# Group-mean subtraction: hand-set semaphores per slot, sums alternating between SBUF and PSUM, and slots moved to multiples of 1 KiB

## Chip, cores, metric

One core of one Trainium2 chip. The metric is device time in microseconds (us) of one execution; a second number, the span, is what the profiler saw inside one execution (about 1.8 us less here). Runs of the kernel before agree within 0.1%.

## The reference

```python
def setup_inputs():
    B, S, D = 8, 4096, 2112
    return {"x": np.random.randn(B, S, D).astype(np.float32)}

def reference(x):                      # stride = 4
    x_r = x.reshape(B, S // stride, stride, D)
    pooled = x_r.mean(axis=2)
    upsampled = np.repeat(pooled, stride, axis=1)
    return (x - upsampled).astype(np.float32)
```

Every group of four rows loses its mean. 276.8 MB have to be read and 276.8 MB written; the arithmetic is small.

## The kernel before

A partition holds one group of four rows: 4 x 2112 float32 values, 33,792 bytes, contiguous both in HBM and in SBUF. A tile is 128 groups; there are 64 tiles. A slot, below, is one of the six tile buffers in SBUF.

```python
STRIDE = 4
IO_BUFS = 6
...
    io_pool = ctx.enter_context(tc.tile_pool(name="io", bufs=IO_BUFS))
    sum_pool = ctx.enter_context(tc.tile_pool(name="sum", bufs=1))

    for g0 in range(0, G, P):
        gsz = min(P, G - g0)
        x_tile = io_pool.tile([P, W], mybir.dt.float32)
        nc.sync.dma_start(out=x_tile[:gsz], in_=xg[g0:g0 + gsz])
        rows = x_tile[:gsz].rearrange("p (f d) -> p f d", f=STRIDE)
        s = sum_pool.tile([P, D], mybir.dt.float32)
        nc.vector.tensor_add(out=s[:gsz], in0=rows[:, 0, :], in1=rows[:, 1, :])
        for f in range(2, STRIDE):
            nc.vector.tensor_add(out=s[:gsz], in0=s[:gsz], in1=rows[:, f, :])
        nc.vector.scalar_tensor_tensor(      # rows = -s/4 + rows, in place
            out=rows, in0=s[:gsz, None, :].to_broadcast([gsz, STRIDE, D]),
            scalar=-1.0 / STRIDE, in1=rows,
            op0=mybir.AluOpType.mult, op1=mybir.AluOpType.add,
        )
        nc.scalar.dma_start(out=og[g0:g0 + gsz], in_=x_tile[:gsz])
```

Loads are issued by SyncE (queue q1 in the profile), stores by ScalarE (queue q10). The tile framework sets all semaphores and chooses the order of VectorE's instructions.

Of the kernel before, what the change touches and what calls it, by code (L numbers as in the profile page):

```python
# [1 line left out]

# [4 lines left out]

STRIDE = 4
IO_BUFS = 6  # L10


@with_exitstack
def kernel(
    ctx: ExitStack,
    tc: tile.TileContext,
    x: bass.AP,
    out: bass.AP,
):



    nc = tc.nc
    B, S, D = x.shape
    P = nc.NUM_PARTITIONS
    assert S % STRIDE == 0
    G = (B * S) // STRIDE
    W = STRIDE * D

    xg = x.rearrange("b (g f) d -> (b g) (f d)", f=STRIDE)  # L30
    og = out.rearrange("b (g f) d -> (b g) (f d)", f=STRIDE)

    io_pool = ctx.enter_context(tc.tile_pool(name="io", bufs=IO_BUFS))
    sum_pool = ctx.enter_context(tc.tile_pool(name="sum", bufs=1))

    for g0 in range(0, G, P):
        gsz = min(P, G - g0)
        x_tile = io_pool.tile([P, W], mybir.dt.float32)
        nc.sync.dma_start(out=x_tile[:gsz], in_=xg[g0:g0 + gsz])

        rows = x_tile[:gsz].rearrange("p (f d) -> p f d", f=STRIDE)
        s = sum_pool.tile([P, D], mybir.dt.float32)
        nc.vector.tensor_add(out=s[:gsz], in0=rows[:, 0, :], in1=rows[:, 1, :])  # L43
        for f in range(2, STRIDE):
            nc.vector.tensor_add(out=s[:gsz], in0=s[:gsz], in1=rows[:, f, :])  # L45
        nc.vector.scalar_tensor_tensor(  # L46
            out=rows,
            in0=s[:gsz, None, :].to_broadcast([gsz, STRIDE, D]),
            scalar=-1.0 / STRIDE,
            in1=rows,  # L50
            op0=mybir.AluOpType.mult,
            op1=mybir.AluOpType.add,
        )
        nc.scalar.dma_start(out=og[g0:g0 + gsz], in_=x_tile[:gsz])


# [1 line left out]
_INS = ['x']  # L58
_OUTS = [((8, 4096, 2112), 'float32')]


# [23 lines left out]
```

## Time and profile before

| | before |
|---|---|
| time, median of 3 | 1286.44 us |
| span | 1284.7 us |
| DMA, mean over the span | 431 GB/s |
| VectorE (DVE) busy | 1026.1 us, 80% |
| VectorE waiting for loads | 237.3 us |

Parts 1 to 3 of the page of the kernel before. In the rows of 40 each digit is the busy share of one slice of the span in tenths.

```profile
span 1284.7 us, 674 instructions
DVE 1026.1 (80%) x256; POOL 0.2 (0%) x4
DVE  5998778787787877878778787787887878778784
DMA  9999999999999999999999999999999999999998
GB/s 404 421 438 438 433 425 437 438 427 432 437 437 426 435 437 431 429 437 437 431 428 438 437 431 429 437 436 432 428 438 436 430 430 437 437 426 433 438 431 380
DMA packets 18437, 553.70 MB, mean 431 GB/s; under 512 B 2048, under 2 KB 2048, under 8 KB 2048
q1 hardware_dynamic: 9216, 276.83, 50.0%
q10 hardware_dynamic: 9216, 276.83, 49.9%
q14 instruction: 5, 0.04, 0.0%
```

The DMA row is at 9 in 39 of 40 slices and the two queues' packets fill the 16 engines' time (50.0% + 49.9%): the DMA engines hardly ever rest. Next, the groups of VectorE instructions (count | busy us, mean ns | idle before and what ended it), then VectorE's waits (total us, times, longest).

```profile
L46 DVE SCALAR_TENSOR_TENSOR x_tile<-s,x_tile 128x8448 f32<-128x8448 f32 x64 | 573.3, 8958 | 2.2
L43 DVE TENSOR_TENSOR s<-x_tile 128x2112 f32<-128x2112 f32 x64 | 150.9, 2358 | 237.5 <-DMA x_tile<-in_x_dram 237.3
L45 DVE TENSOR_TENSOR s<-s,x_tile 128x2112 f32<-128x2112 f32 x128 | 301.8, 2358 | 4.4
```

```profile
DVE s L43 <- DMA x_tile<-in_x_dram: 237.3, 59, 13.1
```

A tile costs VectorE 2.358 + 2 x 2.358 + 8.958 = 16.03 us and the DMA engines 1284.7 / 64 = 20 us. So VectorE waits for loads 59 times, about 4 us per tile, and has that much to spare. One view misleads:

```profile
## 4 chain that ended last, share of the span: by engine, by line
DVE 80%; another core or an unknown queue 17%; DMA 1%; issue 1%; DVEq 0%
```

The chain that ended last runs through VectorE because each of its waits ends with a load. That the load was late because the engines were full is not in the chain; it is in the DMA row.

The packed trace also has every DMA packet's start and duration. From these records: 16,384 data packets of 33,792 bytes, which makes 1024 per engine, from 1.75 us to 1283.56 us. Nearly every one (98.6% within 1 ns) is recorded as 1251 ns long, loads and stores alike.

### The profile page before, as it was taken

How to read it: one execution, taken by the hardware profiler on the slowest of the kernel's cores; microseconds unless marked ns; L12 is line 12 of the kernel's file. 1: busy time of each engine (PE TensorE's matmuls, PEld its weight loads, DVE VectorE, ACT ScalarE, POOL GpSimd, SP SyncE). 2: the span in 40 equal slices, each digit the busy share in tenths (PEclk: the TensorE clock that was granted, in tenths of full speed). 3: DMA queues.
4: the chain of work that ended last, by engine and by line, in shares of the span. 5: the costliest groups of instructions: out<-in, count | busy, mean ns of one | idle time of the engine just before them, and what ended most of it. 6: DMA issues, size and time to landing. Idle time of an engine off the chain costs nothing.

```text
span 1284.7 us, 674 instructions
## 1 busy us (share of the span) xinstructions
DVE 1026.1 (80%) x256; POOL 0.2 (0%) x4
## 2 busy tenths in 40 slices
DVE  5998778787787877878778787787887878778784
POOL 0000000000000000000000000000000000000000
DMA  9999999999999999999999999999999999999998
GB/s 404 421 438 438 433 425 437 438 427 432 437 437 426 435 437 431 429 437 437 431 428 438 437 431 429 437 436 432 428 438 436 430 430 437 437 426 433 438 431 380
DMA packets 18437, 553.70 MB, mean 431 GB/s; under 512 B 2048, under 2 KB 2048, under 8 KB 2048
## 3 DMA queue, kind: packets, MB, share of 16 engines
q1 hardware_dynamic: 9216, 276.83, 50.0%
q10 hardware_dynamic: 9216, 276.83, 49.9%
q14 instruction: 5, 0.04, 0.0%
HBM read 276.82 MB, written 276.82 MB: 431 GB/s over the span
## 4 chain that ended last, share of the span: by engine, by line
DVE 80%; another core or an unknown queue 17%; DMA 1%; issue 1%; DVEq 0%
DVE x_tile L46 45%; DVE s L45 24%; DVE s L43 12%; DMA x_tile<-in_x_dram 1%; DVEq L43 0%
## 5 line engine op out<-in xcount | busy, mean ns | idle before, releaser
L46 DVE SCALAR_TENSOR_TENSOR x_tile<-s,x_tile 128x8448 f32<-128x8448 f32 x64 | 573.3, 8958 | 2.2
L43 DVE TENSOR_TENSOR s<-x_tile 128x2112 f32<-128x2112 f32 x64 | 150.9, 2358 | 237.5 <-DMA x_tile<-in_x_dram 237.3
L45 DVE TENSOR_TENSOR s<-s,x_tile 128x2112 f32<-128x2112 f32 x128 | 301.8, 2358 | 4.4
L69 POOL MEMSET const-bfloat16-1.0<- 128x1 bf16 x1 | 0.1, 103 | 0.0
L69 POOL MEMSET const-uint8-127<- 128x1 uint8 x1 | 0.1, 102 | 0.0
L69 POOL MEMSET const-float32-0.0<- 128x1 f32 x1 | 0.1, 100 | 0.2 <-issue 0.2
L69 POOL MEMSET const-float32-1.0<- 128x1 f32 x1 | 0.1, 99 | 0.0
## 6 DMA issues: line engine op xcount, KB each, us to landing
x_tile<-in_x_dram SPq DMA_DIRECT2D x64, 4224.0 KB, 59.6
out_dram<-x_tile ACTq DMA_DIRECT2D x64, 4224.0 KB, 43.8
```

What stands on the lines that cost most here:

```text
L43: nc.vector.tensor_add(out=s[:gsz], in0=rows[:, 0, :], in1=rows[:, 1, :])
L45: nc.vector.tensor_add(out=s[:gsz], in0=s[:gsz], in1=rows[:, f, :])
L46: nc.vector.scalar_tensor_tensor(out=rows, in0=s[:gsz, None, :].to_broadcast([gsz, STRIDE, D]), scalar=-1.0 / STRIDE, in1=rows, op0=mybir. ...
L69: nc = _bacc.Bacc("TRN2", target_bir_lowering=False, num_devices=1)
```

## The change

Its intent: one fixed program per queue, with one semaphore per slot and direction, so that a load waits for its own slot's store alone; two sum buffers, so that a tile's first add needs no wait for the previous tile's subtraction; and slots at multiples of 1 KiB instead of 128 bytes past a multiple of 256. The second sum buffer lies in PSUM because I took SBUF to have no room for it beside the six slots.

The diff, cut to its core:

```diff
-    for g0 in range(0, G, P):
-        x_tile = io_pool.tile([P, W], mybir.dt.float32)
-        nc.sync.dma_start(out=x_tile[:gsz], in_=xg[g0:g0 + gsz])
-        s = sum_pool.tile([P, D], mybir.dt.float32)
 ...
+    pad_pool.tile([P, PAD], f32, name="pad")                # PAD = 224: 896 bytes
+    slots = [io_pool.tile([P, W], f32, name=f"slot{b}") for b in range(SLOTS)]
+    s_sb = sum_pool.tile([P, D], f32, name="s_sb")
+    s_ps = psum_pool.tile([P, D], f32, name="s_ps")
+    load_sems = [tc.alloc_semaphore(f"load{b}") for b in range(SLOTS)]
+    store_sems = [tc.alloc_semaphore(f"store{b}") for b in range(SLOTS)]
+    done_sem = tc.alloc_semaphore("done")
+    with tc.tile_critical():
+        done = 0
+        for k in range(n):
+            b, lap = k % SLOTS, k // SLOTS
+            s = s_ps if k % 2 else s_sb
+            load = nc.sync.dma_start(out=slots[b][:], in_=xg[tile_rows])
+            if lap:
+                load._wait_ge(store_sems[b], 16 * lap)
+            load.then_inc(load_sems[b], 16)
+            add = nc.vector.tensor_add(out=s[:], in0=rows[:, 0, :], in1=rows[:, 1, :])
+            add._wait_ge(load_sems[b], 16 * (lap + 1))
+            add.then_inc(done_sem)
 ... (two more adds and the subtraction, each waiting for the one before)
+            store = nc.scalar.dma_start(out=og[tile_rows], in_=slots[b][:])
+            store._wait_ge(done_sem, done)
+            store.then_inc(store_sems[b], 16)
+        for b in range(SLOTS):
+            nc.sync.wait_ge(store_sems[b], 16 * len(range(b, n, SLOTS)))
```

More of the change, by code (lines that the diff above doesn't have):

```diff
@@ L9 @@
 STRIDE = 4
-IO_BUFS = 6
+SLOTS = 6
+PAD = 224
 @with_exitstack
@@ L25 @@
     P = nc.NUM_PARTITIONS
-    assert S % STRIDE == 0
+    W = STRIDE * D
     G = (B * S) // STRIDE
-    W = STRIDE * D
+    assert S % STRIDE == 0 and G % P == 0
+    n = G // P
     xg = x.rearrange("b (g f) d -> (b g) (f d)", f=STRIDE)
     og = out.rearrange("b (g f) d -> (b g) (f d)", f=STRIDE)
-    io_pool = ctx.enter_context(tc.tile_pool(name="io", bufs=IO_BUFS))
+    f32 = mybir.dt.float32
+    pad_pool = ctx.enter_context(tc.tile_pool(name="pad", bufs=1))
+    io_pool = ctx.enter_context(tc.tile_pool(name="io", bufs=1))
@@ L34 @@
     sum_pool = ctx.enter_context(tc.tile_pool(name="sum", bufs=1))
-    for g0 in range(0, G, P):
-        gsz = min(P, G - g0)
-        x_tile = io_pool.tile([P, W], mybir.dt.float32)
-        nc.sync.dma_start(out=x_tile[:gsz], in_=xg[g0:g0 + gsz])
-        rows = x_tile[:gsz].rearrange("p (f d) -> p f d", f=STRIDE)
-        s = sum_pool.tile([P, D], mybir.dt.float32)
-        nc.vector.tensor_add(out=s[:gsz], in0=rows[:, 0, :], in1=rows[:, 1, :])
-        for f in range(2, STRIDE):
-            nc.vector.tensor_add(out=s[:gsz], in0=s[:gsz], in1=rows[:, f, :])
-        nc.vector.scalar_tensor_tensor(
-            out=rows,
-            in0=s[:gsz, None, :].to_broadcast([gsz, STRIDE, D]),
-            scalar=-1.0 / STRIDE,
-            in1=rows,
-            op0=mybir.AluOpType.mult,
-            op1=mybir.AluOpType.add,
-        )
-        nc.scalar.dma_start(out=og[g0:g0 + gsz], in_=x_tile[:gsz])
+    psum_pool = ctx.enter_context(
+        tc.tile_pool(name="psum", bufs=1, space=bass.MemoryType.PSUM)
+    )
@@ new lines @@
+    pad_pool.tile([P, PAD], f32, name="pad")
[9 more added lines that the diff above has]
+            b, lap = k % SLOTS, k // SLOTS
+            rows = slots[b].rearrange("p (f d) -> p f d", f=STRIDE)
+            s = s_ps if k % 2 else s_sb
+            tile_rows = slice(k * P, (k + 1) * P)
+            load = nc.sync.dma_start(out=slots[b][:], in_=xg[tile_rows])
[5 more added lines that the diff above has]
+            add.then_inc(done_sem)
+            done += 1
+            for f in range(2, STRIDE):
+                add = nc.vector.tensor_add(out=s[:], in0=s[:], in1=rows[:, f, :])
+                add._wait_ge(done_sem, done)
+                add.then_inc(done_sem)
+                done += 1
+            sub = nc.vector.scalar_tensor_tensor(
+                out=rows,
+                in0=s[:, None, :].to_broadcast([P, STRIDE, D]),
+                scalar=-1.0 / STRIDE,
+                in1=rows,
+                op0=mybir.AluOpType.mult,
+                op1=mybir.AluOpType.add,
+            )
+            sub._wait_ge(done_sem, done)
+            sub.then_inc(done_sem)
+            done += 1
+            store = nc.scalar.dma_start(out=og[tile_rows], in_=slots[b][:])
[3 more added lines that the diff above has]
+            nc.sync.wait_ge(store_sems[b], 16 * len(range(b, n, SLOTS)))
```

## The prediction

The forecast's sum, a gain from aligned slot addresses and a small cost of the critical section, both applied to the 1286.4 us before, came to 1281.7 us if alignment counted for loads and stores ("the first", which the forecast weighs most), to 1284 us if for stores alone, and to 1286.5 us if not at all.

> **What bounds the kernel now.** The DMA engines. The page's DMA row shows 9 in 39 of 40 slices, 431 GB/s; the two queues' packets take 50.0% + 49.9% of the 16 engines' time. In the trace's DMA records 16,384 data packets of 33,792 bytes (one partition row of a tile) run back to back on every engine, from 1.7 to 1283.6 us of a 1284.7 us span. The median packet takes 1251 ns, loads and stores alike; 98% are within 1 ns of it. 1024 packets per engine x 1.251 us = 1281 us: that is the time. Slower packets add about 1.7 us, nearly all in the first 34 us (start, and the first stores).
>
> **What does not.** VectorE works 16.03 us per tile (four instructions, groups view) against 20.0 us of DMA; it waits 237 us for loads (waits view). The chain of waits says "DVE 80%", but its waits end with loads queued behind saturated engines. Load issues wait 1158 us for stores, yet the engines never run dry.
>
> **What the change does.**
> 1. Semaphores per slot instead of eight shared lanes: load k waits only for its slot's store, and six loads start at once rather than five. No engine idle time is there to recover: worth 0 (at most 0.5 us in the first 35 us).
> 2. Sums of odd tiles in PSUM: [...]VectorE has 4 us of slack per tile: worth 0.
> 3. Critical section: branches and a barrier[...].
> 4. Slot addresses. The built programs put the slots at 16,512 + j x 33,792 bytes before, 128 mod 256, and at 17,408 + j x 33,792 after, a multiple of 1024. [...]loads (aligned HBM reads, misaligned SBUF writes) take the same 1251 ns[...].
>
> **Predicted time.** [...]If not: 1286.5. I weigh the first most: 1282.3 us, 80% range 1278.5 to 1287. Faster by over 2%: 0.02; within 2%: 0.96; slower: 0.02. A 2% gain would need 442 GB/s, more than any slice shows (438).
>
> **What would show each step.** [...]DMA row still 9s, 433 GB/s. VectorE's adds with PSUM within 0.1 us of 2.36, its idle time still filled by loads. The first DMA a few tenths later.
>
> **What would make it wrong.** [...]Waiting for one's own slot alone letting a queue run dry so that engines idle, or PSUM operands slowing VectorE past 20 us per tile: slower.[...]

## The result, and the profile after

After: 1286.88 us median of 6 runs (1286.79 to 1287.20); before, same session: 1286.48 us of 6 (1286.44 to 1287.14). Ratio 1.0003, 95% interval 0.999 to 1.0016: the same. Here and below a ratio is the mean time of one kernel's fast runs over that of the other's in the same rounds, so it is not quite the ratio of the medians quoted.

The page of the kernel after, the lines that answer to those above:

```profile
span 1285.0 us, 439 instructions
DVE 1026.5 (80%) x256; POOL 0.2 (0%) x4
DMA  9999999999999999999999999999999999999998
DMA packets 18434, 553.67 MB, mean 431 GB/s; under 512 B 2048, under 2 KB 2048, under 8 KB 2048
q1 hardware_dynamic: 9216, 276.83, 50.0%
q10 hardware_dynamic: 9216, 276.83, 49.9%
q14 instruction: 2, 0.02, 0.0%
```

The DMA row, the volume and the rate are what they were. Groups and waits of VectorE in the kernel after:

```profile
L75 DVE SCALAR_TENSOR_TENSOR slot<-s_sb,slot 128x8448 f32<-128x8448 f32 x32 | 286.7, 8958 | 1.1
L75 DVE SCALAR_TENSOR_TENSOR slot<-s_ps,slot 128x8448 f32<-128x8448 f32 x32 | 286.6, 8957 | 1.1
L66 DVE TENSOR_TENSOR s_sb<-slot 128x2112 f32<-128x2112 f32 x32 | 75.5, 2358 | 123.4 <-DMA slot<-in_x_dram 123.4
L66 DVE TENSOR_TENSOR s_ps<-slot 128x2112 f32<-128x2112 f32 x32 | 75.7, 2367 | 113.0 <-DMA slot<-in_x_dram 113.0
L71 DVE TENSOR_TENSOR s_ps<-s_ps,slot 128x2112 f32<-128x2112 f32 x64 | 151.4, 2366 | 2.2
L71 DVE TENSOR_TENSOR s_sb<-s_sb,slot 128x2112 f32<-128x2112 f32 x64 | 150.9, 2358 | 2.2
```

```profile
DVE s_sb L66 <- DMA slot<-in_x_dram: 123.4, 30, 13.3
DVE s_ps L66 <- DMA slot<-in_x_dram: 113.0, 30, 4.8
```

An add into PSUM takes 8 to 9 ns more than one into SBUF, the subtraction from PSUM 1 ns less, and VectorE still waits 236.4 us for loads. The DMA records show the main point: data packets are still recorded as 1251 ns, on both queues. The gain that I had put on the slot addresses (1281.7 us forecast with it, 1286.5 without) is absent: 1286.88 us.

Those records hold a second number that I had not read: the mean distance from one packet's start to the next on an engine. (The records name no engine. So it is taken as 16 times the slope of a straight line through the starts of all data packets, in order, between 250 and 630 us, a stretch in which neither kernel fetches instructions. It includes the share of the completion writes, packets of 4 bytes: 2048 on each of the two pages, as many as the semaphore updates by DMA in their traces.) It is 1247.8 ns before and 1247.8 ns after. (The 1247.9 ns in the expectations below came from a longer stretch with fetches in it.) Consecutive records thus overlap by 3 ns, and a record's length is not what a packet costs.

### The profile page after: what moved, and what is told of

It reads as the page before. It is cut to its first block, busy times and chain, and to the rows that moved or that the text cites. A ratio compares the mean times of both kernels' runs of the same rounds, so it can differ in the third digit from the quotient of the medians.

```text
span 1285.0 us, 439 instructions
## 1 busy us (share of the span) xinstructions
DVE 1026.5 (80%) x256; POOL 0.2 (0%) x4
## 2 busy tenths in 40 slices
DMA packets 18434, 553.67 MB, mean 431 GB/s; under 512 B 2048, under 2 KB 2048, under 8 KB 2048
## 3 DMA queue, kind: packets, MB, share of 16 engines
q10 hardware_dynamic: 9216, 276.83, 49.9%
## 4 chain that ended last, share of the span: by engine, by line
DVE 80%; another core or an unknown queue 17%; DMA 1%; issue 0%; SPq 0%
DVE slot L75 45%; DVE s_ps L71 12%; DVE s_sb L71 12%; DVE s_ps L66 6%; DVE s_sb L66 6%; DMA slot<-in_x_dram 1%; SPq L118 0%; SPq L53 0%
## 5 line engine op out<-in xcount | busy, mean ns | idle before, releaser
L75 DVE SCALAR_TENSOR_TENSOR slot<-s_sb,slot 128x8448 f32<-128x8448 f32 x32 | 286.7, 8958 | 1.1
L75 DVE SCALAR_TENSOR_TENSOR slot<-s_ps,slot 128x8448 f32<-128x8448 f32 x32 | 286.6, 8957 | 1.1
L66 DVE TENSOR_TENSOR s_sb<-slot 128x2112 f32<-128x2112 f32 x32 | 75.5, 2358 | 123.4 <-DMA slot<-in_x_dram 123.4
L66 DVE TENSOR_TENSOR s_ps<-slot 128x2112 f32<-128x2112 f32 x32 | 75.7, 2367 | 113.0 <-DMA slot<-in_x_dram 113.0
L71 DVE TENSOR_TENSOR s_ps<-s_ps,slot 128x2112 f32<-128x2112 f32 x64 | 151.4, 2366 | 2.2
L71 DVE TENSOR_TENSOR s_sb<-s_sb,slot 128x2112 f32<-128x2112 f32 x64 | 150.9, 2358 | 2.2
```

The lines of the kernel that those rows point to most:

```text
L66: add = nc.vector.tensor_add(out=s[:], in0=rows[:, 0, :], in1=rows[:, 1, :])
L71: add = nc.vector.tensor_add(out=s[:], in0=s[:], in1=rows[:, f, :])
L75: sub = nc.vector.scalar_tensor_tensor(out=rows, in0=s[:, None, :].to_broadcast([P, STRIDE, D]), scalar=-1.0 / STRIDE, in1=rows, op0=mybir ...
```

## The experiments

Theory A: a packet costs its bytes at a fixed rate plus a fixed overhead, and start addresses are worth nothing here. Rival B: alignment did save 5 us and the new synchronisation gave them back. C and D are named where they arise. All edits are to the kernel after unless said otherwise. Runs of one batch share a chip with their runs of the kernel before.

| run | time, us (runs) | before beside it, us | ratio, 95% interval |
|---|---|---|---|
| pad_only | 1286.48 (5) | 1286.54 | 0.9999, 0.9986 to 1.0011 |
| rows_aligned | 1301.05 (4) | 1286.54 | 1.0112, 1.0097 to 1.0128 |
| rows_off128 | 1301.10 (4) | 1286.54 | 1.0112, 1.0099 to 1.0126 |
| rows_off4 | 1301.82 (4) | 1286.54 | 1.0118, 1.0104 to 1.0132 |
| sync_nopad | 1286.79 (5) | 1286.63 | 1.0001, 0.9989 to 1.0013 |
| extra1 | 1287.64 (4) | 1286.63 | 1.0016, 1.0003 to 1.0029 |
| big | 1307.38 (6) | 1286.63 | 1.0145, 1.0111 to 1.0179 |
| hbm_off | 1286.78 (4) | 1286.63 | 1.0001, 0.9987 to 1.0016 |
| psum_only | 1346.11 (6) | 1286.61 | 1.0383, 1.0336 to 1.0431 |
| dma_only | 1285.51 (4) | 1286.61 | 0.9993, 0.998 to 1.0005 |
| extra3 | 1516.03 (1) | 1286.61 | one look |
| slots3 | 1334.90 (1) | 1286.61 | one look |

### pad_only: the address alone, in the kernel before

```diff
+    pad_pool = ctx.enter_context(tc.tile_pool(name="pad", bufs=1))
+    pad_pool.tile([P, 224], mybir.dt.float32, name="pad")
     io_pool = ctx.enter_context(tc.tile_pool(name="io", bufs=IO_BUFS))
```

> The kernel before with the 896-byte pad alone: its slots start at a multiple of 1024 bytes, waits and sums as before. Theory A (a packet costs its bytes plus a fixed overhead, and 128 bytes off a boundary costs nothing): median data packet 1251 ns, time within 0.5 us of 1286.5. Rival B (alignment saves some 5 us but the new synchronisation gave it back): [...]time near 1281.5 us.

1286.48 us, packets 1251 ns long and 1247.8 ns apart. Moving the slots does nothing by itself (1286.54 us beside it without the pad), so there was no gain to give back.

### sync_nopad: the rest of the change without the address

```diff
-PAD = 224
-    pad_pool = ctx.enter_context(tc.tile_pool(name="pad", bufs=1))
-    pad_pool.tile([P, PAD], f32, name="pad")
```

> The kernel after without the pad: slots again 128 bytes off a multiple of 256, everything else new. Theory A (alignment is worth nothing; the 0.3 us longer span of after is the entry and exit of the critical section): packets 1251 ns, spacing 1247.9 ns, span 1285.0 and time 1286.8 us as after. Rival B (pad gained, synchronisation lost): near 1291 us.

1286.79 us, span 1284.9 us, packets 1251 ns long and 1247.8 ns apart. Rival B is dead from both sides.

### rows_aligned, rows_off128, rows_off4: four times as many descriptors, at three alignments

By a descriptor I mean one contiguous row of a transfer; in these runs each shows as one data packet (65,536 rows; the page's 67,586 packets less 2048 completion writes and 2 fetches). Each of a slot's four rows now stands 256 bytes apart from the next, so a tile moves in rows of 8448 bytes (33 x 256) instead of 33,792. Five slots, as I took six of this size not to fit (not shown). OFF is 0, 32 or 1 element, which is 0, 128 or 4 bytes past a multiple of 256.

```diff
-SLOTS = 6
+SLOTS = 5
-    slots = [io_pool.tile([P, W], f32, name=f"slot{b}") for b in range(SLOTS)]
+    RW = D + 64
+    wide = io_pool.tile([P, SLOTS * STRIDE * RW + 64], f32, name="slots")
+    slots = [
+        wide[:, OFF + b * STRIDE * RW:OFF + (b + 1) * STRIDE * RW].rearrange(
+            "p (f r) -> p f r", f=STRIDE
+        )[:, :, 0:D]
+        for b in range(SLOTS)
+    ]
 ... (loads and stores as "p (f d) -> p f d" on the HBM side)
```

> The kernel after with 5 slots, each of its four rows stored apart at multiples of 256 bytes, so that every tile moves in descriptors of 8448 bytes, four times as many. Theory A[...]: packets of 319 ns, about 26 us longer in all, 1312 us. Rival C (1251 ns is a lower rate, without a cost per packet): packets of 313 ns, about 1287 us.

> As rows_aligned, every row 128 bytes off a multiple of 256. Theory A: the same as rows_aligned within 1 us.[...]

> As rows_aligned, every row 4 bytes off a multiple of 256. Theory A in its strong form (no SBUF address costs anything): as rows_aligned within 1 us. Rival D (128 bytes off is aligned enough, the unit is smaller): clearly longer[...].

From the page of rows_aligned:

```profile
span 1299.3 us, 438 instructions
DMA packets 67586, 553.67 MB, mean 426 GB/s; under 512 B 2048, under 2 KB 2048, under 8 KB 2048
q1 hardware_dynamic: 33792, 276.83, 50.4%
q10 hardware_dynamic: 33792, 276.83, 50.3%
```

The packets are four times as many, and their recorded lengths add up to 100.7% of the 16 engines' span: records overlap, and five slots in place of six did not make the engines run dry. The two packet sizes give both constants:

| | 33,792 bytes (after) | 8448 bytes (rows_aligned) | per byte, times 16 engines | left over per packet |
|---|---|---|---|---|
| recorded length, ns | 1251 | 319 | 435.1 GB/s | 8.3 ns |
| start to start, ns | 1247.8 | 315.5 | 434.9 GB/s | 4.7 ns |

(Per byte: the difference of the two columns over 33,792 - 8448 = 25,344 bytes; left over: 315.5 or 319 less 8448 times that. The completion writes, one per 8 packets of the one size and one per 32 of the other, drop out of the 4.7 ns.) So a packet costs its bytes at 435 GB/s and 4.7 ns more. My expectation of 319 ns for the record was met, that of 1312 us was not: it took the recorded overhead of 8.3 ns for the cost. With 4.7 ns, 3072 more packets per engine cost 14.4 us; measured 1301.05 - 1286.88 = 14.2 us. (This checks that the spacing accounts for the time; it is no second measurement of the 4.7 ns, which came from the same runs.) Rival C, a lower rate without a cost per packet, is out.

Start addresses: 1301.05 us aligned, 1301.10 us at 128 bytes, 1301.82 us at 4 bytes. So 128 bytes off cost nothing measurable (0.05 us between the medians), where I had expected a clear cost. Four bytes off cost 0.8 us in all, a spacing of 315.6 instead of 315.5 ns, not the clearly longer time of rival D.

### hbm_off: the other side of the transfer

```diff
+HBM_OFF = 63
+    flat = x.rearrange("b s d -> (b s d)")
-            load = nc.sync.dma_start(out=slots[b][:], in_=xg[tile_rows])
+            at = k * P * W + (HBM_OFF if k < n - 1 else 0)
+            src = flat[at:at + P * W].rearrange("(p w) -> p w", p=P)
+            load = nc.sync.dma_start(out=slots[b][:], in_=src)
```

> The kernel after, its loads (but the last) shifted by 63 elements in HBM, 252 bytes off a multiple of 256; wrong results on purpose. [...]Theory A extended to HBM (start addresses cost nothing in rows this long): 1251 ns, 1286.9 us.

1286.78 us, wrong results, load packets still 1251 ns. HBM reads that start 252 bytes past a multiple of 256 cost the same in rows of this length. HBM writes off a boundary were not tried.

### extra1, extra3: how much slack has VectorE?

```diff
             add._wait_ge(load_sems[b], 16 * (lap + 1))
             add.then_inc(done_sem)
             done += 1
+            for _ in range(1):          # 3 in extra3
+                add = nc.vector.tensor_add(out=s[:], in0=rows[:, 0, :], in1=rows[:, 1, :])
+                add._wait_ge(done_sem, done)
+                add.then_inc(done_sem)
+                done += 1
```

> The kernel after with the first add done twice: VectorE 18.4 us per tile against 20.0 us of DMA. If VectorE is off the critical path: time within 1 us of after's 1286.9, VectorE's wait for loads about 151 us shorter (64 x 2.36) than 236 us. If VectorE bounds it, as the chain of waits' 80% suggests at a first look: about 151 us longer, 1438 us.

> The kernel after with the first add done four times: VectorE about 23.2 us per tile, over the 20.0 us of DMA. The limit should change over: 13 us before the first add + 64 x 23.2 + some 12 us for the last store: 1505 to 1515 us, DMA row at 8, VectorE no longer waiting for loads.

The page and the waits of extra1, then the page of extra3:

```profile
span 1285.8 us, 503 instructions
DVE 1176.8 (92%) x320; POOL 0.2 (0%) x4
```

```profile
DVE s_sb L66 <- DMA slot<-in_x_dram: 48.1, 25, 13.4
DVE s_ps L66 <- DMA slot<-in_x_dram: 36.6, 25, 2.4
```

```profile
span 1514.3 us, 631 instructions
DVE 1474.7 (97%) x448; POOL 0.2 (0%) x4
DMA  9999989899899999999999989989999989999535
```

With one more add VectorE works 150.3 us longer, waits 151.7 us less (84.7 us), and the median time rises by 0.8 us; one of its four runs took 1292.0 us, for a reason not known. With three more, VectorE needs 23.2 us per tile, the limit changes over, and the kernel takes 1516 us, 1 us outside what I had expected. Note the trap in the DMA row of extra3: it still shows mostly 9, where I had expected 8, although the rate on its page is down to 366 GB/s. Near a full row the rate and the packet spacing tell more than the busy share.

### dma_only: no VectorE work at all

```diff
 ... (the three adds and the subtraction removed)
-            store._wait_ge(done_sem, done)
+            store._wait_ge(load_sems[b], 16 * (lap + 1))
```

> The kernel after without any VectorE work: each tile is stored as it was loaded, wrong results on purpose. If the DMA engines alone set the time: the same 1286 to 1287 us, spacing 1247.9 ns. If 1026 us of VectorE work costs anything (sharing of SBUF, late stores): several us shorter.

1285.51 us, wrong results, packets 1247.8 ns apart. 1026 us of VectorE work add 1.4 us to the time of 1285.5 us. This is just below what I had expected, and the records point to where the rest went. The profile's queue q14 fetches instructions in packets of 8192 bytes, and each fetch during the run coincides within 0.3 us with one longer data packet:

| | fetches during the transfers | data packets over 1400 ns after 40 us | first packet to last, us |
|---|---|---|---|
| dma_only | 0 | 0 | 1279.75 |
| after | 2 | 2 (1788, 1787 ns) | 1281.04 |
| extra1 | 3 | 3 | 1281.77 |
| before | 5 | 5 (1495 to 1788 ns) | 1281.82 |

The completion records say the same in another way. Take for each transfer the time from its first to its last engine's completion. In the kernel before it is 0.3 to 0.4 us until the fetch at 218 us, about 1.0 us from then on, 1.9 us after the fetch at 638 us and 2.7 us after that at 1063 us. In the kernel after it steps from 0.5 to 1.1 us after the fetch at 206 us and to 1.9 us after that at 845 us. In dma_only it stays between 0.47 and 0.61 us throughout. So an engine that is delayed hardly catches up, as one would expect where packets fill the engines' time (50.0% + 49.9% on the pages of before and after). The last transfer is 0.54 us wide in dma_only and 1.77 us in after: that is 1.2 of the 1.3 us between their first-to-last times.

So VectorE's data traffic costs nothing measurable in the spacing (1247.8 ns with it and without); each of the two lengthened packets in after (1788 and 1787 ns in place of 1251) stands beside a fetch of instructions. The steps in time are shown; that the fetches cause them is inferred, as no run changed the fetches alone.

### big: fewer, larger packets?

Two groups per partition (rows of 67,584 bytes) and 3 slots; the last tile is stored in two halves.

```diff
-SLOTS = 6
+SLOTS = 3
+GROUPS = 2
-    W = STRIDE * D
+    W = GROUPS * STRIDE * D
 ... (VectorE's four instructions once per group)
```

> The kernel after with two groups per partition row, so DMA rows of 67,584 bytes, and 3 slots. Theory A (4.7 ns per packet[...], from the spacing of rows_aligned and after): if such a row moves as one packet, spacing 2490 ns per packet and about 2.4 us less in the steady part; head and tail are coarser (one store of half a tile after the last load), so 1284 to 1290 us in all. If the row is cut into pieces of the old size or smaller: no gain per byte. Rival C (a rate, no cost per packet): nothing gained.

1307.38 us, scattered from 1295.75 to 1311.56. The data packets number 16,384 and are 33,792 bytes, as before: each row was cut in two. No packet was saved, so the case of "no gain per byte" applied. The time rose by 20 us besides; that the three coarse slots are the reason is likely, not shown.

### slots3: three slots of the old size

```diff
-SLOTS = 6
+SLOTS = 3
```

> The kernel after with 3 slots of the old size: one slot with VectorE leaves two tiles for the DMA engines. If the engines only need one transfer pending at any time: within 10 us of 1287. If latency from issue to first packet (1 us at the start, 5 us from the first store's issue to its first packet) is exposed once per tile: 64 x 1 to 5 us longer, 1350 us and over.

1334.9 us in one look, between my two bands. 48 us over 64 tiles is 0.75 us per tile; the mean packet spacing between 60 and 1200 us rises to 1285.8 ns, and the page reads 415 GB/s. Six slots do hide something that three do not; how much of it is first-packet latency this run does not tell.

### psum_only: the alternation alone, left to the framework

```diff
+    psum_pool = ctx.enter_context(
+        tc.tile_pool(name="psum", bufs=1, space=bass.MemoryType.PSUM)
+    )
-        s = sum_pool.tile([P, D], mybir.dt.float32)
+        s = (psum_pool if (g0 // P) % 2 else sum_pool).tile([P, D], mybir.dt.float32)
```

> The kernel before with its sums alternating between SBUF and PSUM, waits and addresses as before. VectorE off the critical path: adds into PSUM near 2366 ns, time within 0.5 us of 1286.5, first packet near 1.75 us and 1.2 us from the last packet to the end of the span (as before, so that the later start and end of after belong to the critical section). Rival: the sums buffer was a hidden coupling, and time falls by over 1 us.

This was the surprise: 1346.11 us, from 1327.6 to 1356.0. (The profiled run took 1327.6 us. Three of the six runs count as slow by the rule of 1.5% over the kernel's own fastest; the three fast ones are 1327.6, 1343.8 and 1328.1 us, and all are far above before.) The instructions are no slower (means of 2363, 2354 and 8952 ns, against 2358, 2358 and 8958 in before). Timeline of psum_only in the middle of the run: start, duration, instruction, and the idle time before it.

```profile
93.82 2.37 DVE L46 TENSOR_TENSOR s<-x_tile 128x2112 f32<-128x2112 f32 x1 [1.91 <-DMA x_tile<-in_x_dram]
96.09 8.95 DVE L49 SCALAR_TENSOR_TENSOR x_tile<-s,x_tile 128x8448 f32<-128x8448 f32 x1
104.96 2.36 DVE L48 TENSOR_TENSOR s<-s,x_tile 128x2112 f32<-128x2112 f32 x1
113.87 2.36 DVE L46 TENSOR_TENSOR s<-x_tile 128x2112 f32<-128x2112 f32 x1 [6.54 <-DMA x_tile<-in_x_dram]
116.14 4.62 DVE L48 TENSOR_TENSOR s<-s,x_tile 128x2112 f32<-128x2112 f32 x2
120.67 8.95 DVE L49 SCALAR_TENSOR_TENSOR x_tile<-s,x_tile 128x8448 f32<-128x8448 f32 x1
129.54 2.35 DVE L48 TENSOR_TENSOR s<-s,x_tile 128x2112 f32<-128x2112 f32 x1
```

And the kernel after, a stretch of the same kind:

```profile
114.19 2.36 DVE L66 TENSOR_TENSOR s_sb<-slot 128x2112 f32<-128x2112 f32 x1 [3.79 <-DMA slot<-in_x_dram]
116.58 4.75 DVE L71 TENSOR_TENSOR s_sb<-s_sb,slot 128x2112 f32<-128x2112 f32 x2
121.37 8.96 DVE L75 SCALAR_TENSOR_TENSOR slot<-s_sb,slot 128x8448 f32<-128x8448 f32 x1
134.16 2.37 DVE L66 TENSOR_TENSOR s_ps<-slot 128x2112 f32<-128x2112 f32 x1 [3.83 <-DMA slot<-in_x_dram]
```

After finishes a tile before it looks at the next. In psum_only the framework, no longer held by a single sum buffer, interleaved two tiles: the first add of tile k+1 (113.87) stands before the subtraction of tile k (120.67). So a tile that has landed is not subtracted and stored until the next one has landed as well. Windows of psum_only (stretch, length, then busy time of DVE and POOL, clock, DMA share, GB/s):

```profile
40.00:700.00 660.00, 522.51 (x134) 0.00 (x0) 1.00 1.00 433
700.00:1250.00 550.00, 405.39 (x104) 0.00 (x0) 1.00 1.00 421
1250.00:1326.00 76.00, 55.12 (x13) 0.00 (x0) 1.00 0.62 264
```

For 700 us the full rate holds (433 GB/s). Then it sags (421, then 264 GB/s) and the end is a string of single stores. In the completion records the distance from a transfer's first engine to its last is 2 us at 650 us, hardly more than in before (1.9 us). Then it grows instead of standing still: the loads are 3 us wide at 700 us, 17 us at 900 us and 41 to 47 us after 1050 us, about two tiles' time; the stores reach some 10 us. From 750 us on, data packets of over 1400 ns appear by the dozen, on both queues. (In each kernel such packets also stand at the very start and shortly after the first store's issue, in before at 1.8 to 2.4 and 31 to 33 us.) So the engines run apart, and a tile waits for the last of its transfer's 16 completions (2048 for 128 transfers in before). One would then expect faster engines to run short of work. The records do not show this before the end: from 700 to 1250 us lengths over 1251 ns add up to 13.9 us per engine, and gaps (fewer than 16 packets in flight) to 1.8 us only. Whether a long record hides a wait, the trace does not tell. How the small lag of 2 us is amplified, and why the time differs from run to run, stays open. That the order of the instructions is the cause is argued: psum_only and before differ in that order, in where half the sums lie, and in how the framework dealt the transfers to its eight semaphores; and sync_nopad has sums in PSUM with the order kept and takes 1286.79 us; but it also has other semaphores, so the order was not changed alone.

## Why the prediction was right or wrong

The forecast of "within 2%" and the bottleneck were right. The time, 1286.88 us, fell at the upper edge of the range (1278.5 to 1287) and 4.6 us above the point, because one step failed. That the median lies inside, by 0.1 us, is luck (two of the six runs took over 1287). That the range reached so far is not: the prediction had named this outcome, "If not: 1286.5", and weighed it too low.

1. **What bounds the kernel: right.** dma_only takes 1285.5 us without any arithmetic, and extra1 adds 150 us of VectorE work for 0.8 us.
2. **Semaphores per slot, "worth 0": right.** sync_nopad shows 1286.79 us. What the prediction did not see is that the hand-set program fixes VectorE's order, and that the alternation may need this: left to the framework, it cost at least 41 us.
3. **Sums in PSUM, "worth 0": right for the change.** Adds cost 8 to 9 ns more (2366 and 2367 ns against 2358).
4. **Critical section: more than I had allowed, but mostly hidden.** The first data packet starts at 1.95 us instead of 1.75 (+0.20) and the span ends 2.04 us after the last packet instead of 1.16 (+0.88). In the two runs of the kernel before with a small edit and no critical section, pad_only and psum_only, these are 1.7 and 1.16 us as before. The end is shorter with fewer slots (1.57 us with three in slots3), so the final waits, one per slot, seem to be part of it. Against that the transfers take 1281.04 instead of 1281.82 us (-0.77), beside 2 instruction fetches where there were 5 (dma_only shows why that may count). The sum, +0.31 us, is the difference of the spans.
5. **Slot addresses, 1281.7 us with a gain from them: wrong.** This is the step that failed. The gain was my estimate, worked out from figures that no run here shows; that they added up to the measured 1251 ns was coincidence. The 8.3 ns that a record has beyond its bytes were taken for misalignment plus a small overhead; the two packet sizes show them to be a property of every packet, aligned or not, and only 4.7 ns of them cost time. The prediction named this alternative, an overhead on every packet, and weighed it too low. There was evidence to weigh: loads and stores had the same 1251 ns although only the stores read from misaligned addresses, and the completion writes of 4 bytes were recorded as 9 ns, nearly all of which is overhead too.

What the time consists of, from the records of the kernel after: 1024 packets at 1247.8 ns are 1277.7 us, of which 1024 x 4.7 = 4.8 us are overhead; slower packets, mostly in the first 34 us, take 1.6 us; the rest is the first and last 2 us, engines that finish apart, and 1.8 us outside the span. No version tried that gives right results beats the kernel before beyond the noise, and the bytes alone at 435 GB/s are 1273 us, 1.1% below.

## What to carry to other kernels

Where the DMA row is full, read the packet spacing, and compare two packet sizes to split it into a rate and an overhead, before believing in a cost worked out from one size (here 1251 ns, 8.3 ns of it beyond the bytes, of which 4.7 ns cost time); one number that matches proves nothing when two sums of small terms give it. Here fewer waits and freer buffers bought nothing, as no DMA engine had idled for lack of them. And a second buffer given to a scheduler is also freedom to reorder: look at the order of the instructions, because a store that waits for the next load may be what cost psum_only its 41 us and more.
